# State-space products of a group: two runs of 14 with double-buffered decay matrices, or one run of 28 with four tiles

## The chip, the core and the metric

The kernel runs on one core of a Trainium2 chip. The time is that of the device for one execution, in microseconds. Before the change three runs took 1905.84, 1906.14 and 1908.29 us; the median is 1906.14.

## What is computed

Two transformer-like blocks run one after the other over 512 positions of width 1024. The change lies in the second block, in its state-space branch: 32 heads of width 64 in 8 groups of 4 heads; the heads of a group share two matrices B and C with 128 states. In the reference, cut to what matters:

```python
seg = a_cs[..., :, None] - a_cs[..., None, :]
decay_in = jnp.exp(jnp.where(causal, seg, -jnp.inf))
cb = jnp.einsum("bclgn,bcsgn->bgcls", c_mat, b_mat)
y_diag = jnp.einsum("bgcls,bgrcls,bcsgrp->bclgrp", cb, decay_in, xdt)
...
y_off = jnp.einsum("bclgn,bcgrpn,bgrcl->bclgrp", c_mat, prev, jnp.exp(a_cs))
y = y_diag + y_off + x * d_skip.reshape(G, R)[..., None]
```

So for every chunk and head there is a product of the inputs with a matrix "scores of B and C times the head's decay", and a product of C with the state carried in from the chunk before, scaled by a decay.

## The kernel before, in words

The second block keeps channels on the 128 partitions and positions on the free axis. Its large products go through `gemm_tile`: a weight block of 128 x 1024 values is loaded on SyncE's queue (`wr`, three buffers), split by ScalarE (`wh`, line 138) and VectorE (`wl`, line 139) into a high and a low part, and TensorE does three products of 128 x 512 for each of its eight slices (lines 150 to 152) into one of three accumulator banks (`acc`).

The state-space branch goes over 8 groups. For each group the loop calls `group_a` (line 873, the part that changes), then `group_in` for the next group (four gemms and short convolutions: two input tiles `xt`, B and C), the two gemms of a gated convolution, `z_in` (two gemms), one or two gate gemms, and `group_b`, which gates and normalises. The long convolution of 30 VectorE steps (line 826) is dealt out in the background.

`group_a` works with chunks of 128 positions, four of them. It transposes B and `xt` (lines 880, 887), scales the transposed inputs (`xd`, `xw`, line 891), forms the scores of B and C and masks them (`cb`, lines 897, 899), and builds the three carried states (`st`, lines 905 to 912). These use the two banks of the pool `mA`. Then it treats the heads in two pairs (e = 0, 1). For each head r of the pair a row of cumulated decays is loaded and broadcast to all partitions by a DMA on GpSimd's queue (`ab`, line 920, two buffers); ScalarE takes four Relus (line 924) and one Exp into another tile (`mt`, line 925, two buffers); VectorE multiplies by `cb` in place (line 926). A run of 14 products follows (line 935): 8 of `xd` with the factors into the bank `psd`, and 6 of C with the states into the bank `pso_`; both banks come from the pool `mB`, which has two. The two heads of a pair write the two halves of the partitions, so each product uses a tile of 128 x 64. Then VectorE assembles the pair's result `y` (lines 943 to 945), with a factor `ep` that a DMA loads (line 941).

The order of the work on each engine is fixed before the run by a planner: it simulates the engines with a cost model and gives each engine the ready instruction that was written first, or that has a raised priority (weight splitting has). `keep_in_program_order` ties an instruction behind the one written before it on its engine, so a run keeps its inner order; other products may still be placed between its members. A buffer of a tile's tag is given again when the last reader of its former content is done.

Of the kernel before, what the change touches and what calls it, by code (L numbers as in the profile page):

```python
# [6 lines left out]
F32 = mybir.dt.float32  # L7
# [3 lines left out]
AF = mybir.ActivationFunctionType  # L11
ALU = mybir.AluOpType
# [4 lines left out]
P = 128  # L17
# [51 lines left out]
def _build(tc, nc, es, a, out):  # L69
    V, A, T, G = nc.vector, nc.scalar, nc.tensor, nc.gpsimd  # L70
# [15 lines left out]
    def mA():  # L86
        return psa.tile([P, S], F32, tag="pa", name="pa")

    def mB():
        return psb.tile([P, S], F32, tag="pb", name="pb")  # L90
# [17 lines left out]
    mt = []  # L108
# [19 lines left out]
    def vcol(name, i=0, n=1):  # L128
        c, k = VEC[name]
        assert i + n <= k  # L130
        return vec[:, c + i:c + i + n]
# [146 lines left out]
    with es_mx:  # L278
# [6 lines left out]
        with tc.high_priority(2000):  # L285
            for k in range(0, 8, 2):
                c = slice(k, k + 2)
# [43 lines left out]
    with ExitStack() as ea:  # L331
# [9 lines left out]
        with ExitStack() as er:  # L341
# [11 lines left out]
                                 op0=ALU.mult, op1=ALU.add)  # L353
# [63 lines left out]
        ab = lambda i, j: 4 * i + j - i  # L417

        def hgrn_in(i):
            psf = gemm_tile([(a["w_gf"][i], 8)], xs)  # L420
            q = ph.tile([P, S], F32, tag="q", name="q")
            k_ = ph.tile([P, S], F32, tag="k", name="k")
            f = ph.tile([P, S], F32, tag="f", name="f")
            A.activation(out=f, in_=psf, func=AF.Sigmoid)
            psq = gemm_tile([(a["w_gq"][i], 8)], xs)
            sg = ph.tile([P, S], F32, tag="t", name="sg")
            A.activation(out=sg, in_=psq, func=AF.Sigmoid)
            V.tensor_scalar(out=f, in0=f, scalar1=oml[:, i:i + 1], scalar2=lb[:, i:i + 1], op0=ALU.mult, op1=ALU.add)
            V.tensor_scalar(out=k_, in0=f, scalar1=-1.0, scalar2=1.0, op0=ALU.mult, op1=ALU.add)
            V.tensor_tensor(out=q, in0=psq, in1=sg, op=ALU.mult)  # L430
            return q, k_, f
# [157 lines left out]
        hd = [hgrn_in(0), hgrn_in(1)]  # L589
# [7 lines left out]
        hd = [hgrn_in(2), hgrn_in(3)]  # L597
# [144 lines left out]
    acc_ = pdt.tile([P, 4, 32], F32, tag="acc_", name="acc_")  # L742
    wc = pdt.tile([P, 4, 32], F32, tag="wc", name="wc")
    cdb = pdt.tile([P, 32, 4], F32, tag="cdb", name="cdb")
    acsd = dram.tile([32, S], F32, tag="acsd", name="acsd")
# [127 lines left out]
    def group_a(g, xt, B, C):  # L873

        pg = pools["pg"]

        Bt = pg.tile([P, 3, P], F32, tag="Btok", name="Btok")
        ps = mA()
        for c in range(3):
            T.transpose(out=ps[:, c * P:(c + 1) * P], in_=B[:, c * P:(c + 1) * P], identity=ident)  # L880
        A.copy(out=Bt.rearrange("p a b -> p (a b)"), in_=ps[:, 0:3 * P])
        xd = pg.tile([P, 4, 4, 64], F32, tag="xd", name="xd")
        xw = pg.tile([P, 3, 4, 64], F32, tag="xw", name="xw")
        for e in range(2):
            ps = mA()
            for c in range(4):
                T.transpose(out=ps[:, c * P:(c + 1) * P], in_=xt[e][:, c * P:(c + 1) * P], identity=ident)  # L887
            pv = ps.rearrange("p (c r d) -> p c r d", r=2, d=64)
            hh = 4 * g + 2 * e
            for dst, sc, n in ((xd, dtc, 4), (xw, wc, 3)):  # L890
                V.tensor_tensor(out=dst[:, :, 2 * e:2 * e + 2, :], in0=pv[:, 0:n],
                                in1=sc[:, 0:n, hh:hh + 2].unsqueeze(3).to_broadcast([P, n, 2, 64]), op=ALU.mult)

        ps = mA()
        for c in range(4):
            sl = slice(c * P, (c + 1) * P)
            T.matmul(out=ps[:, sl], lhsT=B[:, sl], rhs=C[:, sl], start=True, stop=True)  # L897
        cb = pg.tile([P, 4, P], F32, tag="cb", name="cb")
        V.tensor_tensor(out=cb, in0=ps.rearrange("p (c l) -> p c l", l=P), in1=tri.unsqueeze(1).to_broadcast([P, 4, P]),
                        op=ALU.mult)  # L900

        st = pg.tile([P, 3, 256], F32, tag="st", name="st")
        for c in range(3):
            ps = mA()
            T.matmul(out=ps[:, 0:256], lhsT=Bt[:, c, :], rhs=xw[:, c].rearrange("p r d -> p (r d)"), start=True, stop=True)  # L905
            if c == 0:
                A.copy(out=st[:, 0, :], in_=ps[:, 0:256])
            else:
                V.tensor_tensor(out=st[:, c, :].rearrange("p (r d) -> p r d", d=64),
                                in0=st[:, c - 1, :].rearrange("p (r d) -> p r d", d=64),  # L910
                                in1=cdb[:, 4 * g:4 * g + 4, c].unsqueeze(2).to_broadcast([P, 4, 64]), op=ALU.mult)
                V.tensor_tensor(out=st[:, c, :], in0=st[:, c, :], in1=ps[:, 0:256], op=ALU.add)
        ys = []
        for e in range(2):
            psd = mB()
            mts = []
            for r in range(2):
                hd = 4 * g + 2 * e + r
                ab_ = pg.tile([P, 4, P], F32, tag="ab", name="ab", bufs=2)
                G.dma_start(out=ab_.rearrange("p a b -> p (a b)"), in_=acsd[hd:hd + 1, :].partition_broadcast(P))  # L920
                mt = pg.tile([P, 4, P], F32, tag="mt", name="mt", bufs=2)

                for c in range(4):
                    A.activation(out=ab_[:, c, :], in_=ab_[:, c, :], func=AF.Relu, scale=-1.0, bias=acc_[:, c, hd:hd + 1])
                A.activation(out=mt, in_=ab_, func=AF.Exp, scale=-1.0)
                V.tensor_tensor(out=mt, in0=mt, in1=cb, op=ALU.mult)
                mts.append(mt)


            pso_ = mB()  # L930
            run = [(psd, c, xd[:, c, 2 * e + r, :], mts[r][:, c, :], r) for c in range(4) for r in (1, 0)]
            run += [(pso_, c, st[:, c - 1, e * P + r * 64:e * P + r * 64 + 64], C[:, c * P:(c + 1) * P], r)
                    for c in range(1, 4) for r in (1, 0)]
            for i, (dst, c, lh, rh, r) in enumerate(run):
                m = T.matmul(out=dst[r * 64:r * 64 + 64, c * P:(c + 1) * P], lhsT=lh, rhs=rh, start=True, stop=True)  # L935
                if i:
                    tc.keep_in_program_order(m)
            ep = pg.tile([P, 3 * P], F32, tag="ep", name="ep", bufs=1)
            for r in range(2):
                hd = 4 * g + 2 * e + r  # L940
                G.dma_start(out=ep[r * 64:r * 64 + 64, :], in_=eacd[hd:hd + 1, P:].partition_broadcast(64))
            y = pg.tile([P, S], F32, tag="y", name="y", bufs=2)
            V.scalar_tensor_tensor(out=y, in0=xt[e], scalar=vcol("d_skip_2", 2 * g + e), in1=psd, op0=ALU.mult, op1=ALU.add)
            V.tensor_tensor(out=ep, in0=pso_[:, P:], in1=ep, op=ALU.mult)
            V.tensor_tensor(out=y[:, P:], in0=y[:, P:], in1=ep, op=ALU.add)
            ys.append(y)
        return ys
# [58 lines left out]
    for g in range(8):  # L1006
        ys = group_a(g, *cur)
        bg(BG[1])
        if g < 7:
            cur = group_in(g + 1)  # L1010
        bgq.append(conv31(g, glu(g)))
        bg(BG[3])
        zs = z_in(g)
        for _ in range(GPG[g]):
            gate_d(gq.pop(0))
            bg(BG[5])
        if g == 4:
            ssm_half(0, yn)
            yn = []
        yn += group_b(g, ys, zs)  # L1020
        bg(BG[6])
# [241 lines left out]
```

## Time and profile before

| what | value |
|---|---|
| median of three runs | 1906.14 us |
| profiled execution | 1905.93 us |
| its span, first to last instruction | 1904.2 us |
| TensorE matmul busy | 1882.7 us, 99% |
| VectorE busy | 1206.9 us, 63% |
| ScalarE busy | 861.9 us, 45% |
| GpSimd busy | 107.2 us, 6% |
| DMA, mean over the span | 111 GB/s |

Shares are of the span. PE is TensorE's matmul, PEld its weight load, DVE is VectorE, ACT is ScalarE, POOL is GpSimd. Matmuls are pipelined and their ends are modelled, so distances between starts tell more than durations. The state-space loop lies at about 855 to 1340 us of the span.

### The profile page before, as it was taken

To read this page: it belongs to the slowest core of one execution; us is meant where nothing else is said; L and a number is where in the kernel's file an instruction comes from. 1 tells how busy PE (TensorE), PEld (TensorE's weight loads), DVE (VectorE), ACT (ScalarE), POOL (GpSimd) and SP (SyncE) were. 2 spreads that over 40 slices of the span, in tenths; PEclk is the share of its full clock that TensorE was granted. 3 is DMA by queue.
4 is the path that set the end of the run, shared out by engine and by line. 5 is a ranking of instruction groups with operands and counts; after the bars stand their busy time and mean duration, and the time that the engine had idled before them with its cause. 6 is when DMAs were issued, how large, how long until landed. Compare 5 with 4: busy or idle time off the path is not lost.

```text
span 1904.2 us, 24959 instructions
## 1 busy us (share of the span) xinstructions
PE 1882.7 (99%) x9601; PEld 1563.1 (82%) x9601; DVE 1206.9 (63%) x1884; ACT 861.9 (45%) x1402; POOL 107.2 (6%) x207
## 2 busy tenths in 40 slices
PE   9999999999999999999999999999999999999997
PEld 8887776878888888877888888888888988888897
DVE  6744756665442344477988988579997764324456
ACT  6524556443431243358544663555344642232244
POOL 1001110000000000011110110110000000000000
PEclk9999999999999999999999999999999999999998
DMA  7312222312233223334433333332345522232244
GB/s 261 133 56 100 67 67 89 100 56 89 89 99 97 93 99 111 113 86 142 136 119 117 114 125 105 114 117 97 121 141 174 173 94 93 84 112 100 93 132 142
DMA packets 68511, 211.74 MB, mean 111 GB/s; under 512 B 8757, under 2 KB 15713, under 8 KB 68393
## 3 DMA queue, kind: packets, MB, share of 16 engines
q1 hardware_dynamic: 57856, 184.09, 29.4%
q0 software_dynamic: 6848, 19.75, 3.4%
q10 hardware_dynamic: 3688, 6.32, 1.0%
q8 instruction: 76, 1.25, 0.3%
q14 instruction: 43, 0.34, 0.1%
HBM read 201.59 MB, written 8.56 MB: 110 GB/s over the span
## 4 chain that ended last, share of the span: by engine, by line
PE 51%; issue 2%; DVE 1%; ACT 0%; DMA 0%; POOL 0%; POOLq 0%; DVEq 0%; ACTq 0%
PE acc L150 16%; PE acc L152 16%; PE acc L151 16%; PE pb L935 1%; PE pa L905 1%; PE pa L897 0%; PE pa L887 0%; PE pc L223 0%; DMA ab<-acsd 0%; PE pa L238 0%; PE pa L223 0%; POOL rc L231 0%; DVE yl L202 0%; PE pa L880 0%; DVE f L1175 0%
## 5 line engine op out<-in xcount | busy, mean ns | idle before, releaser
L138 ACT CAST wh<-wr 128x1024 fp32r<-128x1024 f32 (+1 forms) x343 | 347.2, 1013 | 720.8 <-PE acc L151 592.9
L139 DVE TENSOR_TENSOR wl<-wr,wh 128x1024 fp32r<-128x1024 f32 (+1 forms) x343 | 403.3, 1176 | 292.2 <-ACT wh L138 285.3
L150 PE MATMUL acc<-yh,wh 128*128 128x512 f32 (+1 forms) x1112 | 432.4, 389 | 0.4 <-DVE so L983 0.3
L152 PE MATMUL acc<-yh,wl 128*128 128x512 f32 (+1 forms) x1112 | 431.5, 388 | 0.0
L151 PE MATMUL acc<-yl,wh 128*128 128x512 f32 (+1 forms) x1112 | 429.8, 387 | 0.0
L152 PE MATMUL acc<-xh,wl 128*128 128x512 f32 (+1 forms) x832 | 314.4, 378 | 0.3 <-DVE wl L139 0.3
L151 PE MATMUL acc<-xl,wh 128*128 128x512 f32 (+1 forms) x832 | 313.5, 377 | 0.0
L150 PE MATMUL acc<-xh,wh 128*128 128x512 f32 (+1 forms) x832 | 313.1, 377 | 0.3 <-DVE h L613 0.3
L150 PEld LDWEIGHTS acc<-yh,wh 128*128 128x128 f32 x1112 | 209.1, 188 | 42.5 <-issue 1.4
L152 PEld LDWEIGHTS acc<-yh,wl 128*128 128x128 f32 x1112 | 209.0, 188 | 42.0 <-issue 1.2
L151 PEld LDWEIGHTS acc<-yl,wh 128*128 128x128 f32 x1112 | 209.1, 188 | 41.5 <-issue 1.1
L150 PE MATMUL acc<-uh,wh 128*128 128x512 f32 (+1 forms) x520 | 183.9, 354 | 0.0
L152 PE MATMUL acc<-uh,wl 128*128 128x512 f32 (+1 forms) x520 | 183.7, 353 | 0.0
L151 PE MATMUL acc<-ul,wh 128*128 128x512 f32 (+1 forms) x520 | 183.7, 353 | 0.0
L826 DVE SCALAR_TENSOR_TENSOR cv<-gp,vec,cv 128x512 f32<-128x512 f32 x240 | 177.9, 748 | 5.9 <-ACT cv L824 3.0
L152 PEld LDWEIGHTS acc<-xh,wl 128*128 128x128 f32 x832 | 157.3, 189 | 28.9 <-issue 2.4
L150 PEld LDWEIGHTS acc<-xh,wh 128*128 128x128 f32 x832 | 157.1, 189 | 28.6 <-ACT xh L201 0.9
L151 PEld LDWEIGHTS acc<-xl,wh 128*128 128x128 f32 x832 | 157.0, 189 | 27.3 <-issue 1.3
L150 PEld LDWEIGHTS acc<-uh,wh 128*128 128x128 f32 x520 | 98.3, 189 | 13.6
L152 PEld LDWEIGHTS acc<-uh,wl 128*128 128x128 f32 x520 | 98.3, 189 | 13.4
L151 PEld LDWEIGHTS acc<-ul,wh 128*128 128x128 f32 x520 | 98.3, 189 | 13.4
L231 POOL TENSOR_TENSOR rc<-rv,mhalf 128x4 f32<-128x4 f32 (+2 forms) x23 | 27.1, 1178 | 961.5 <-DVE rv L229 876.1
(370 smaller groups left out, 2095.8 us busy)
## 6 DMA issues: line engine op xcount, KB each, us to landing
wr<-w SPq DMA_DIRECT2D x64, 512.0 KB, 3.7
wr<-w_gu SPq DMA_DIRECT2D x44, 512.0 KB, 3.5
wr<-w_out SPq DMA_DIRECT2D x24, 512.0 KB, 3.5
wr<-w_dn SPq DMA_DIRECT2D x24, 512.0 KB, 3.5
wr<-w_xs SPq DMA_DIRECT2D x16, 512.0 KB, 3.5
wr<-w_glu SPq DMA_DIRECT2D x16, 512.0 KB, 3.8
ab<-acsd POOLq DMA_DIRECT2D x32, 256.0 KB, 3.8
wr<-w_z SPq DMA_DIRECT2D x16, 512.0 KB, 3.8
```

The costliest lines, as they stand in the source:

```text
L138: A.copy(out=hi[:, :n], in_=raw[:, :n])
L139: V.tensor_tensor(out=lo[:, :n], in0=raw[:, :n], in1=hi[:, :n].bitcast(F32), op=ALU.subtract)
L150: T.matmul(out=ps, lhsT=lh, rhs=rh, start=start, stop=False)
L151: T.matmul(out=ps, lhsT=lh, rhs=rl, start=False, stop=False)
L152: T.matmul(out=ps, lhsT=ll, rhs=rh, start=False, stop=stop)
L231: G.tensor_tensor(out=r[:, :nt], in0=v[:, :nt], in1=mhalf[:, :nt], op=ALU.pow)
L826: yield V.scalar_tensor_tensor(out=o, in0=gp[:, t:t + S], scalar=cw(t), in1=o, op0=ALU.mult, op1=ALU.add)
L905: T.matmul(out=ps[:, 0:256], lhsT=Bt[:, c, :], rhs=xw[:, c].rearrange("p r d -> p (r d)"), start=True, stop=True)
L935: m = T.matmul(out=dst[r * 64:r * 64 + 64, c * P:(c + 1) * P], lhsT=lh, rhs=rh, start=True, stop=True)
```

## The change

The four heads' decay matrices are worked out first, each in one tile of four (`ab`, four buffers; the tag `mt` is gone): load, Relu, Exp and multiplication all in place. Then one run has the products of all four heads: 16 products with the factors and 12 with the states, the pair e = 1 ahead of e = 0 in either part. The results go to four banks: the factor products to the two of `mB`, the state products to the two of `mA`. The loads of `ep` and the assembly of `y` follow for both pairs.

```diff
+        mts = []
+        for i in range(4):
+            hd = 4 * g + i
+            mt = pg.tile([P, 4, P], F32, tag="ab", name="ab", bufs=4)
+            G.dma_start(out=mt.rearrange("p a b -> p (a b)"), in_=acsd[hd:hd + 1, :].partition_broadcast(P))
+
+            for c in range(4):
+                A.activation(out=mt[:, c, :], in_=mt[:, c, :], func=AF.Relu, scale=-1.0, bias=acc_[:, c, hd:hd + 1])
+            A.activation(out=mt, in_=mt, func=AF.Exp, scale=-1.0)
+            V.tensor_tensor(out=mt, in0=mt, in1=cb, op=ALU.mult)
+            mts.append(mt)
+
+
+        psd, pso_ = [mB(), mB()], [mA(), mA()]
+        run = [(psd[e], c, xd[:, c, 2 * e + r, :], mts[2 * e + r][:, c, :], r)
+               for e in (1, 0) for c in range(4) for r in (1, 0)]
+        run += [(pso_[e], c, st[:, c - 1, e * P + r * 64:e * P + r * 64 + 64], C[:, c * P:(c + 1) * P], r)
+                for e in (1, 0) for c in range(1, 4) for r in (1, 0)]
+        for i, (dst, c, lh, rh, r) in enumerate(run):
+            m = T.matmul(out=dst[r * 64:r * 64 + 64, c * P:(c + 1) * P], lhsT=lh, rhs=rh, start=True, stop=True)
+            if i:
+                tc.keep_in_program_order(m)
         ys = []
         for e in range(2):
-            psd = mB()
-            mts = []
-            for r in range(2):
-                hd = 4 * g + 2 * e + r
-                ab_ = pg.tile([P, 4, P], F32, tag="ab", name="ab", bufs=2)
-                G.dma_start(out=ab_.rearrange("p a b -> p (a b)"), in_=acsd[hd:hd + 1, :].partition_broadcast(P))
-                mt = pg.tile([P, 4, P], F32, tag="mt", name="mt", bufs=2)
...
-            pso_ = mB()
-            run = [(psd, c, xd[:, c, 2 * e + r, :], mts[r][:, c, :], r) for c in range(4) for r in (1, 0)]
-            run += [(pso_, c, st[:, c - 1, e * P + r * 64:e * P + r * 64 + 64], C[:, c * P:(c + 1) * P], r)
-                    for c in range(1, 4) for r in (1, 0)]
...
-            V.scalar_tensor_tensor(out=y, in0=xt[e], scalar=vcol("d_skip_2", 2 * g + e), in1=psd, op0=ALU.mult, op1=ALU.add)
-            V.tensor_tensor(out=ep, in0=pso_[:, P:], in1=ep, op=ALU.mult)
+            V.scalar_tensor_tensor(out=y, in0=xt[e], scalar=vcol("d_skip_2", 2 * g + e), in1=psd[e], op0=ALU.mult, op1=ALU.add)
+            V.tensor_tensor(out=ep, in0=pso_[e][:, P:], in1=ep, op=ALU.mult)
```

## Rows read from the trace of the kernel before

**Rows 1.** The page: busy time by engine, granted TensorE clock in 40 slices.
```profile
PE 1882.7 (99%) x9601; PEld 1563.1 (82%) x9601; DVE 1206.9 (63%) x1884; ACT 861.9 (45%) x1402; POOL 107.2 (6%) x207
...
PEclk9999999999999999999999999999999999999998
```
**Rows 2.** TensorE's waits, 850 to 1345 us: who, for whom, total, times, longest.
```profile
PE pa L880 <- ACT Bt L804: 1.4, 1, 1.4
```
**Rows 3.** Line 935: instructions, ns min/median/max, first and last start, shapes.
```profile
L935 PE MATMUL pb<-mt,xd x256: 272/273/324, 874.2 to 1334.3; 128*64 128x128 f32 x128
...
L935 PE MATMUL pb<-Ct,st x192: 272/273/323, 875.1 to 1334.9; 128*64 128x128 f32 x192
```
**Rows 4.** Timeline (start, us, instruction): TensorE, gemm alone, 20 starts apart.
```profile
895.31 0.39 PE L150 MATMUL acc<-yh,wh 128*128 128x512 f32 x1
...
899.84 0.39 PE L152 MATMUL acc<-yh,wl 128*128 128x512 f32 x1
```
**Rows 5.** Timeline, TensorE, the runs of the first group.
```profile
875.12 0.61 PE L935 MATMUL pb<-Ct,st 128*64 128x128 f32 x8
...
875.99 0.39 PE L151 MATMUL acc<-yl,wh 128*128 128x512 f32 x1
...
877.15 0.39 PE L150 MATMUL acc<-yh,wh 128*128 128x512 f32 x1
877.47 0.44 PE L935 MATMUL pb<-Ct,st 128*64 128x128 f32 x4
...
878.17 0.39 PE L152 MATMUL acc<-yh,wl 128*128 128x512 f32 x1
...
880.47 0.39 PE L150 MATMUL acc<-yh,wh 128*128 128x512 f32 x1
880.78 1.09 PE L935 MATMUL pb<-mt,xd 128*64 128x128 f32 x16
881.71 0.82 PE L935 MATMUL pb<-Ct,st 128*64 128x128 f32 x12
...
882.80 0.39 PE L152 MATMUL acc<-yh,wl 128*128 128x512 f32 x1
```
**Rows 6.** Timeline, TensorE, the third group (980 to 1043 us).
```profile
986.95 0.40 PE L152 MATMUL acc<-yh,wl 128*128 128x512 f32 x1
987.28 1.09 PE L935 MATMUL pb<-mt,xd 128*64 128x128 f32 x16
...
988.96 0.50 PE L150 MATMUL acc<-yh,wh 128*128 128x512 f32 x1
...
991.82 1.09 PE L935 MATMUL pb<-mt,xd 128*64 128x128 f32 x16
```
**Rows 7.** Timeline, VectorE, the third group.
```profile
986.22 0.68 DVE L926 TENSOR_TENSOR mt<-mt,cb 128x512 f32<-128x512 f32 x1
...
987.80 0.42 DVE L912 TENSOR_TENSOR st<-st,pa 128x256 f32<-128x256 f32 x1
...
990.17 1.29 DVE L926 TENSOR_TENSOR mt<-mt,cb 128x512 f32<-128x512 f32 x2
```
**Rows 8.** Timeline, ScalarE, the third group; in brackets idle before and who ended it.
```profile
986.98 1.28 ACT L925 ACT_TABLE_LOAD   x1 [1.17 <-DVE mt L926]
988.41 1.16 ACT L925 ACTIVATE mt<-ab 128x512 f32<-128x512 f32 x2
...
993.33 1.27 ACT L924 ACTIVATE ab<-ab,acc__6602 128x128 f32<-128x128 f32 x4
...
996.84 0.63 ACT L925 ACTIVATE mt<-ab 128x512 f32<-128x512 f32 x1
997.49 1.28 ACT L804 ACT_TABLE_LOAD   x1
```
**Rows 9.** ScalarE's waits, 850 to 1345 us.
```profile
ACT wh L138 <- PE acc L151: 100.8, 49, 3.9
...
ACT ab L924 <- DMA ab<-acsd: 9.4, 9, 2.0
```
**Rows 10.** Timeline, GpSimd's queue, the third group.
```profile
989.34 0.60 POOL L920 DMA_DIRECT2D ab<-acsd  x1 [2.48 <-ACT mt L925]
```

More of the change, by code (lines that the diff above doesn't have):

```diff
@@ L913, in group_a @@
         ys = []
         for e in range(2):
-            psd = mB()
-            mts = []
-            for r in range(2):
-                hd = 4 * g + 2 * e + r
-                ab_ = pg.tile([P, 4, P], F32, tag="ab", name="ab", bufs=2)
-                G.dma_start(out=ab_.rearrange("p a b -> p (a b)"), in_=acsd[hd:hd + 1, :].partition_broadcast(P))
-                mt = pg.tile([P, 4, P], F32, tag="mt", name="mt", bufs=2)
[L923 to L927, printed above, removed]
@@ L930, in group_a @@
-            pso_ = mB()
-            run = [(psd, c, xd[:, c, 2 * e + r, :], mts[r][:, c, :], r) for c in range(4) for r in (1, 0)]
-            run += [(pso_, c, st[:, c - 1, e * P + r * 64:e * P + r * 64 + 64], C[:, c * P:(c + 1) * P], r)
-                    for c in range(1, 4) for r in (1, 0)]
[L934 to L937, printed above, removed]
```

## The prediction

> **What bounds the kernel now.** I read the busy shares first: TensorE is busy for 1882.7 of 1904.2 us and is granted full clock in nearly every slice [rows 1]. So an edit counts only by what it takes out of TensorE's own stream or puts into it as a gap. Next I read TensorE's waits in the state-space stage alone (850 to 1345 us): one of 1.4 us in the first group, where the transposes of B wait for its Silu, and one of 0.2 us that has no row here [rows 2]. All else the change touches (VectorE, ScalarE, GpSimd, DMA) works under cover there. Then I read line 935, the products of the heads: 256 + 192 = 448 instructions [rows 3]. A traced product of the source stands as two instructions, so these are 16 runs of 14 products, 28 instructions each; 15 stand whole, and the first one stands in two pieces, 24 + 4, with gemm products in between, so TensorE enters and leaves this kind of product 17 times. Last I read the timeline around single runs, where the reader is to look at starts only, since a matmul's end is modelled.
>
> **What one entry and exit costs.** Far from any run, gemm products start every (899.84 - 895.31)/20 = 0.2265 us [rows 4]. In the first group, from the gemm product ahead of a run to the second gemm product behind it, the whole run of 28 takes 882.80 - 880.47 = 2.33 us, the short piece of 4 takes 878.17 - 877.15 = 1.02 us [rows 5]. Their difference, 1.31 us for 24 instructions, is 0.0546 us for each; what is left of the short one is 1.02 - 4 x 0.0546 - 2 x 0.2265 = 0.35 us. This does not depend on the length of the run. The passage inside a run from the factor products to the state products (Ct) shows no such step: 16 instructions in 881.71 - 880.78 = 0.93 us, against 16 x 0.0546 = 0.87, and the 0.05 belongs to the entry. Behind the exit the gemm products limp a little: 875.99 to 877.15 is five steps in 1.16 us, 0.03 more than 5 x 0.2265. So one entry and exit is worth 0.38 us.
>
> Is that 0.35 a change of shape or a wait for data? The products' tile is 128\*64, the gemm's 128\*128. At 880.78 and at 877.47 nothing was being waited for by the timeline, and both pay the full sum; the runs of later groups, 987.28 among them, start 0.33 us behind the last gemm product, hardly more than the 0.31 to 0.32 of those two [rows 5, 6]. So at least nine tenths of it are the change of shape. The Trainium skill, page "TensorEngine Tiling (Array Packing)", section Tiling Modes, Key Properties, says that changing the tiling mode drains the engine while changing only the tile does not; by that rule merging runs saves the switches and nothing inside them, and the trace agrees: the passage inside a run is free.
>
> **The change part by part.**
> *Runs merged.* 17 entries and exits become 8, if each run of 28 products (56 instructions) stays whole: 9 x 0.38 = 3.4 us off TensorE's stream. The products' number and shape stay, 448 x 0.0546 = 24.5 us before and after. If switches vary as the measured ones do, 0.35 to 0.39, the term is 3.2 to 3.5.
>
> *One wait for four factors.* The first product of the new run reads the last factor (e = 1, r = 1), so one wait stands ahead of 56 instructions and of every gemm product queued behind them. Today the first run starts at 987.28, 0.38 us after its second factor ended at 986.90; the second pair's multiplications take 1.29 us, ended at 991.46, and the second run started at 991.82 [rows 6, 7]. Today's second pair is late because its Exp waits for the factor tiles that the first run reads: the table load at 986.98 and two Exps at 988.41 [rows 8]. With four tiles worked in place these Exps can be done long before, as today's first pair is, whose Exps stand at 995 to 997 for a run 50 us later. The run can then start some 1.3 us behind today's first, about 988.6, and 3 us ahead of today's second. TensorE needs 1.3 us of other work there; today it has 988.96 to 991.82, 2.9 us of gemm and one transpose, between the two runs, and only its place changes. I take zero. Bounds: below, zero, since there is no idle there to win back; above, 1.29 us for each of the 8 groups if the planner leaves the run where the first stands today, 10.3 us. I go by zero, since in all 16 present runs the planner's order met the data without a gap.
>
> *State products.* They read a state whose last addition ended at 988.22 [rows 7]; in the new run 32 instructions (1.75 us) come ahead of them. Cost zero; if the planner thinks the state late, as it did in the first group (row with x8), gemm products come in between and the run breaks: 0.38 us for each of 8, up to 3.0 us.
>
> *Banks.* The state products' results move to the pool that the transposes, the score products and the state updates use. The last of these is read by 988.22, ahead of the run, and the next use is the next group's transposes, 60 us on. Nothing else in the loop asks for that pool. Zero; if a bank is late it is the same break, 0.38 a group.
>
> *Loads.* All four 256 KB broadcasts of a group are freed by one run, and are issued together from GpSimd's queue, at 0.6 us each; today they come one by one, each released by an Exp, the first at 989.34 after 2.48 us of waiting in that queue [rows 10]. They will wait for TensorE instead. Behind them in that queue stand the loads of ep, the broadcast of the group norm and small memsets; TensorE waits for none of them in this stage today [rows 2]. ScalarE already waits for these broadcasts, 9.4 us in 9 times, longest 2.0 [rows 9]. More of that stays covered: ScalarE's weight casts wait for TensorE 100.8 us in 49 times [rows 9], so ScalarE is ahead of the products by whole blocks. Zero, bounds -1.4 (the idle of the first group goes) to +4.5 (below).
>
> *Tables.* Four Exps instead of two lie outside the run's neighbourhood, and between them Silu of the next group's convolutions. Today's one pair of loads a group (986.98 and 997.49, 1.28 us each) may become two pairs: 2.57 us more of ScalarE a group, where it has 100.8 us of waiting over 8 groups. I take zero. The Trainium skill, page "ScalarE: Activation LUTs", section What ACT_TABLE_LOAD costs, puts a switch at about 2.66 us, 1.28 for the load and 1.38 for a drain, and speaks against scattering Exps; the load agrees, the drain does not: the load at 997.49 starts 0.02 us behind the end of the Exp (996.84 + 0.63) [rows 8]. By the Trainium skill's figure a second pair would be 5.3 us a group; the measured one decides.
>
> **Sum.** The profiled execution took 1905.93 us, 1.73 outside its span; less 3.4 is 1902.5. It lies 0.2 below the median of the three runs shown; on the median, 1906.14 - 3.4 = 1902.7. What a measurement of this kernel can tell from no change is 0.2%, 3.8 us, so the gain as worked out stays just inside it.
>
> **Rivals.**
> *Broken runs.* The planner puts gemm products between the two parts of every run: 1902.7 + 8 x 0.38 = 1905.7. For it: the first group did that. Against: 15 of 16 did not, and more work now lies ahead of the state products. 12%.
>
> *The one wait (slower).* The run is queued about where today's first run stands and TensorE stands for the second pair of factors: 8 x 1.29 = 10.3 us, 1913.0. The gain is gone from 0.43 us of standing a group; slower by over 0.2% from 0.9. For it: one instruction holds 56, and the order is fixed ahead of time. Against: no present run shows a gap. 8%.
>
> *First group.* There ScalarE gates TensorE [rows 2], the broadcasts land late, and four heads' work is free to start. If one head's four Relus (1.27), an Exp (0.63) and two loads (2.57) come ahead of the Silu of B, TensorE stands 4.5 us longer: 1907.2. Against: program order gives the Silus the earlier place. 8%. The other way, the order shifts so that the 1.4 us of idle goes: 1901.3. 12%.
>
> *Nothing hidden shows:* eight whole runs, no new gap: 1902.7, itself 1902.0 to 1903.4. 60%.
>
> **How the numbers follow.** Broken runs, the forecast and the better first group make 84%; 1900.8 to 1906.2 holds them with half a microsecond to spare, and I take off 4% for shifts of the planner's order that I can't price. Faster by over 0.2% means below 1902.33: the better first group and a third of the forecast's own range, 0.32. Slower means above 1909.95: the one wait, and a little for unpriced shifts, 0.10. The rest, 0.58, is within.
>
> **What would show it.** Line 935 in 8 unbroken stretches of 56, each from the gemm product ahead to the second behind in 0.35 + 56 x 0.0546 + 0.453 = 3.86 us; no TensorE wait for VectorE's line 926; Exps of all four heads ahead of the score products; the second pair of multiplications directly behind the first on VectorE. Wrong: stretches of 32 and 24, a TensorE idle ended by VectorE's factor at the head of a run, or a longer idle ahead of the first transposes of B.

## The result, and the profile after

The changed kernel takes 1918.98 us (median of 4 runs, 1918.58 to 1919.11), the kernel before 1905.99: the ratio is 1.0065, with a 95% interval of 1.0049 to 1.0081. So it is slower by some 13 us, where 3.4 us of gain was forecast. The profiled execution took 1919.06 us, 13.13 more than that of before.

The page's busy row answers to [rows 1]; ScalarE grew by 912.9 - 861.9 = 51.0 us.

```profile
PE 1886.7 (98%) x9601; PEld 1570.4 (82%) x9601; DVE 1206.4 (63%) x1884; ACT 912.9 (48%) x1442; POOL 107.3 (6%) x207
```

TensorE's waits from 850 to 1460 us (who, for whom, us in total, times, longest; two under 0.5 are left out). The kernel before has one of 1.4 us [rows 2] and, behind 1345 us, two of 0.3 and 0.4:

```profile
PE pc L223 <- DVE sqa L215: 3.7, 2, 2.5
PE acc L150 <- ACT xt L800: 3.2, 1, 3.2
PE pa L880 <- ACT Bt L804: 2.4, 1, 2.4
PE acc L150 <- ACT wh L138: 1.5, 1, 1.5
```

The run itself went nearly as worked out. It is line 932 now; the timeline of TensorE (start, us) in the third group, which answers to [rows 6]:

```profile
996.05 0.48 PE L151 MATMUL acc<-yl,wh 128*128 128x512 f32 x1
996.46 1.97 PE L932 MATMUL pb<-ab,xd 128*64 128x128 f32 x32
998.26 1.48 PE L932 MATMUL pa<-Ct,st 128*64 128x128 f32 x24
999.67 0.50 PE L152 MATMUL acc<-yh,wl 128*128 128x512 f32 x1
1000.01 0.40 PE L150 MATMUL acc<-yh,wh 128*128 128x512 f32 x1
```

All eight runs stand whole, 56 instructions each. From the gemm product ahead (996.05) to the second behind (1000.01) are 3.96 us, where 3.86 was worked out; the products from 996.46 to 999.67 are 3.21 of it, 56 x 0.0546 = 3.06 and 0.15. To see what a group gains, I lay the two traces side by side at the first transpose of B (line 880) of each group; the figure is its start in the changed kernel less that in the kernel before, in us:

| | first group | 2nd | 7th | 8th | end of span |
|---|---|---|---|---|---|
| changed kernel | 1.71 | 7.58 | 5.70 | 9.70 | 13.13 |
| e1 (below) | 0.38 | -1.09 | -2.20 | -2.59 | 0.69 |
| e2 (below) | 1.41 | 1.44 | -0.44 | -0.81 | 4.90 |
| e4 (below) | -0.55 | 3.59 | 2.11 | 1.74 | 5.29 |
| e8 (below) | -0.01 | -1.49 | -3.27 | -3.66 | -4.48 |
| e10 (below) | -0.51 | 3.76 | 1.89 | 4.58 | 4.85 |
| e11 (below) | 0.69 | 0.64 | -1.24 | -1.64 | -0.86 |

From the second group to the seventh the changed kernel gains 1.88 us in five groups, 0.376 each: one entry and exit less in each, as forecast (0.38). The loss is in three places: 5.9 us between the first and second group's transposes, with 1.1 more ahead of them; 4.0 in the seventh; 3.4 in the eighth and behind it.

In the first group TensorE waits for a bank that ScalarE empties late, and then the run of 56 takes 885.96 - 881.21 = 4.75 us where it takes 3.21 elsewhere:

```profile
869.88 0.55 PE L880 MATMUL pa<-ident,Bt 128*128 128x128 f32 x3 [2.42 <-ACT Bt L804]
...
880.71 0.57 PE L150 MATMUL acc<-yh,wh 128*128 128x512 f32 x1 [3.16 <-ACT xt L800]
881.21 3.52 PE L932 MATMUL pb<-ab,xd 128*64 128x128 f32 x32
884.55 1.48 PE L932 MATMUL pa<-Ct,st 128*64 128x128 f32 x24
885.96 0.50 PE L151 MATMUL acc<-yl,wh 128*128 128x512 f32 x1
```

The run is longer because of the clock. Busy time by stretch, changed kernel; the third figure from the right is the granted clock:

```profile
870.80:874.10 3.30, 3.30 (x13) 2.67 (x12) 2.31 (x4) 3.27 (x7) 0.00 (x0) 0.50 0.43 151
881.10:884.30 3.20, 3.20 (x31) 3.10 (x32) 2.83 (x4) 2.29 (x4) 0.82 (x2) 0.50 0.39 148
884.50:887.80 3.30, 3.30 (x36) 2.82 (x33) 3.00 (x6) 2.13 (x6) 1.17 (x4) 1.00 0.73 232
1273.60:1276.90 3.30, 3.30 (x11) 2.72 (x11) 2.61 (x5) 0.12 (x1) 0.10 (x1) 0.50 0.35 113
1335.00:1338.30 3.30, 3.30 (x14) 2.91 (x13) 1.68 (x4) 0.00 (x0) 0.00 (x0) 0.50 0.50 161
```

Behind each of four idles in the stage TensorE ran 3.41 us at the lower level, 1.2 GHz (870.77 to 874.18, 881.01 to 884.42, 1273.54 to 1276.95, 1334.98 to 1338.39): some 1.7 us more per idle, an estimate from half the stretch; the run above lost 1.54 in one. The account: new idles 1.07 + 3.16 + 2.52 + 1.17 + 1.13 = 9.05 (the first is 2.42 less the 1.35 of before, the last, 1.45 at 1443 us, less 0.32), half clock 4 x 1.7 = 6.8, merged runs -3.4, and 0.65 that the profiled runs differed by ahead of the stage: 13.1.

Who made ScalarE and VectorE late? In the first group it is not the number of table loads: as in the kernel before, two stand there ahead of the run (865.62 and 871.61; before 863.90 and 869.90). Two other things changed. The first decay load, one of four issued together now, took longer to land (7.3 us from its issue, before 5.7), so ScalarE started later (before, then changed kernel):

```profile
861.79 1.57 ACT L924 ACTIVATE ab<-ab,acc__6602 128x128 f32<-128x128 f32 x5 [2.01 <-DMA ab<-acsd]
```
```profile
863.50 1.58 ACT L920 ACTIVATE ab<-ab,acc__6602 128x128 f32<-128x128 f32 x5 [3.08 <-DMA ab<-acsd]
```

That is the 1.07 us more of idle ahead of the transposes. And the third and fourth head's Exps and the fourth head's Relus now stand ahead of the reading at line 800 that empties the gemm's bank; this is the idle of 3.16 us. Before, the third Exp came at 875.37, behind that reading. ScalarE, before and changed:

```profile
873.33 0.78 ACT L800 ACTIVATE xt<-acc,vec 128x512 f32<-128x512 f32 x1
```
```profile
879.36 0.63 ACT L921 ACTIVATE ab<-ab 128x512 f32<-128x512 f32 x1
879.89 0.76 ACT L800 ACTIVATE xt<-acc,vec 128x512 f32<-128x512 f32 x1
```

In the later groups the table loads come in. Those from 850 to 1345 us, changed kernel (count, busy us, mean ns, idle before them); before there were 9 at line 925 and 9 at line 804:

```profile
L921 ACT ACT_TABLE_LOAD x29 | 37.2, 1283 | 0.5
L804 ACT ACT_TABLE_LOAD x22 | 28.2, 1283 | 0.3
L869 ACT ACT_TABLE_LOAD x8 | 10.3, 1283 | 0.1
```

59 instead of 18: 41 x 1.283 = 52.6 us, and the busy row grew by 51.0. In the third group's period ScalarE has eight of them, where [rows 8] had two (the first two and the last are shown):

```profile
1004.52 1.28 ACT L921 ACT_TABLE_LOAD   x1
1005.82 0.64 ACT L921 ACTIVATE ab<-ab 128x512 f32<-128x512 f32 x1
...
1006.98 1.28 ACT L804 ACT_TABLE_LOAD   x1
...
1035.33 1.28 ACT L869 ACT_TABLE_LOAD   x1
```

From the second group to the sixth they cost TensorE nothing, as the gain of 0.376 a group shows. Ahead of the seventh group's transposes the slack was used up: ScalarE comes later to line 824, VectorE works on its result and is late with the squares (`sqa`), and TensorE waits for these at line 223. Changed kernel, then before:

```profile
1258.35 1.28 ACT L921 ACT_TABLE_LOAD   x1
...
1260.18 0.80 ACT L824 ACTIVATE cv<-gp,vec 128x512 f32<-128x512 f32 x1
1271.87 0.69 DVE L215 TENSOR_TENSOR sqa<-sqa,sq 128x512 f32<-128x512 f32 x1
1272.61 1.05 PE L223 MATMUL pc<-ones,sqa 128*128 128x1 f32 x8 [2.52 <-DVE sqa L215]
```
```profile
1250.06 0.82 ACT L824 ACTIVATE cv<-gp,vec 128x512 f32<-128x512 f32 x1 [1.31 <-DVE gp L817]
1262.55 0.69 DVE L215 TENSOR_TENSOR sqa<-sqa,sq 128x512 f32<-128x512 f32 x1
```

TensorE's own lag is 5.7 us there; line 824 lags by 10.1 and `sqa` by 9.3.

The four Exps now stand one by one between the Silus of the next group's convolutions (line 804) and of z (line 869). Before, an Exp could not go ahead until one of two `mt` tiles was free, which kept Exps together around the runs; four tiles in place are all free behind the run, and the planner puts each Exp where ScalarE is ready for it. That reason is read from the code and the order; no run varies the number of tiles alone. ScalarE's slack, its waits from 850 to 1345 us, fell with it against [rows 9]:

```profile
ACT wh L138 <- PE acc L151: 46.1, 16, 3.9
...
ACT ab L920 <- DMA ab<-acsd: 24.6, 7, 4.3
```

### The profile page after: what moved, and what is told of

It reads as the page before. It is cut to its first block, busy times and chain, and to the rows that moved or that the text cites. A ratio compares the mean times of both kernels' runs of the same rounds, so it can differ in the third digit from the quotient of the medians.

```text
span 1917.3 us, 24971 instructions
## 1 busy us (share of the span) xinstructions
PE 1886.7 (98%) x9601; PEld 1570.4 (82%) x9601; DVE 1206.4 (63%) x1884; ACT 912.9 (48%) x1442; POOL 107.3 (6%) x207
## 4 chain that ended last, share of the span: by engine, by line
PE 46%; issue 3%; DVE 3%; ACT 2%; DMA 1%; POOL 0%; POOLq 0%; DVEq 0%; ACTq 0%
PE acc L150 14%; PE acc L152 14%; PE acc L151 14%; PE pb L932 1%; DVE cv L826 1%; DVE wl L139 1%; PE pa L905 1%; PE pa L932 1%; ACT wh L138 0%; PE pa L897 0%; PE pa L887 0%; DMA ab<-acsd 0%; PE pc L223 0%; ACT cv L1038 0%; PE pa L238 0%
```

## The experiments

All edits are to the changed kernel; ratios are to the kernel before, run on the same chip, with their 95% interval. The theories at the start: A, the scattered Exps (their table loads hold ScalarE, and that TensorE); B, the four loads issued at once; C, the merged run. They ran on several chips, and the kernel before took 1905.0 to 1905.5 us beside them.

**e1: the Exps kept together.** Each Exp is tied behind the copy of the group's first state, which stands shortly ahead of the run.

```diff
-                A.copy(out=st[:, 0, :], in_=ps[:, 0:256])
+                cp = A.copy(out=st[:, 0, :], in_=ps[:, 0:256])
...
-            A.activation(out=mt, in_=mt, func=AF.Exp, scale=-1.0)
+            with tc.issue_after(cp.ins):
+                A.activation(out=mt, in_=mt, func=AF.Exp, scale=-1.0)
```

> The changed kernel with one thing more: the four Exps of every group are tied behind the copy of the group's first state on ScalarE (the copy at line 907), so they can't be placed among the next group's Silus. Theory A (the scattered Exps bring 41 more table loads, 1.283 us each, and these hold ScalarE up where TensorE depends on it): 18 table loads in the state-space stage instead of 59, the TensorE idles of 2.5, 1.2 and 1.5 us in the last two groups and behind the loop shrink to those of the kernel before, the saving of 0.38 us a run stays: 1902 to 1905 us (up to 1907 if the four Exps right ahead of the run make it wait). Rival B (the four loads freed together by one run land late, and ScalarE waits for them): loads are as bunched as before, so 1912 or more. Rival C (the single run of 28 and its one wait): 1915 or more.

1906.62 us, ratio 1.0011 (1.0002 to 1.0020): 12.4 of the 13 us come back. 16 table loads are left in the stage, and the first group's and the seventh's loss are gone. From the second group's transposes on, the gain is 0.36 to 0.39 in each group but the third, where a wait of 0.47 us for VectorE at line 897 takes it away. So the scattered Exps are shown as the cause there; whether by their loads or by their places, this run can't tell. But from the eighth group's transposes to its run's end 4.4 us are lost, so that none of the gain is left. VectorE's `sqa` and TensorE behind it, timelines of e1:

```profile
1320.69 0.69 DVE L215 TENSOR_TENSOR sqa<-sqa,sq 128x512 f32<-128x512 f32 x1
```
```profile
1321.44 1.05 PE L223 MATMUL pc<-ones,sqa 128*128 128x1 f32 x8 [2.19 <-DVE sqa L215]
```

VectorE is late, TensorE stands 2.19 us, and has half clock from 1323.5 to 1327.0.

**e2: no table loads, same places.** Tanh stands in for Exp, so the decay matrices are not the reference's; the other instructions stay, and the table need not change.

```diff
-            A.activation(out=mt, in_=mt, func=AF.Exp, scale=-1.0)
+            A.activation(out=mt, in_=mt, func=AF.Tanh, scale=-1.0)
```

> The changed kernel with Tanh in place of Exp at line 921, so that it needs no other table than Silu and Tanh (the decay matrices are then not those of the reference). Loads, Relus, run and banks stay. Theory A: hardly a table load is left in the state-space stage, ScalarE is 50 us less busy than in the changed kernel, and the time falls to 1901 to 1906 us, with what the first group still loses. Rival B: 1915 or more, since the loads stay bunched. Rival C: 1915 or more, since the run stays.

1909.21 us, 1.0023 (1.0012 to 1.0033); one table load is left in the stage. 9.8 us come back: the seventh group's loss is gone, and of the first group's two idles of 2.4 and 3.2 us there are left 1.8 and 1.1, with no half clock behind them. But Tanh removes 17 table loads that the kernel before has too, so the 9.8 us are not the price of the 41 new ones alone. The 3 us above what was expected are again in the last group: line 223 waits 2.0 us there, with half clock behind it, for 6.83 us this time.

**e3: four tiles in place, but two runs of 14.** The runs are written as before the change, with their banks from `mB`.

```diff
+            psd[e], pso_[e] = mB(), mB()
+            run = [(psd[e], c, xd[:, c, 2 * e + r, :], mts[2 * e + r][:, c, :], r) for c in range(4) for r in (1, 0)]
```

> The changed kernel with the merged run alone undone: four tiles in place, all four heads worked out first, but two runs of 14 products into the banks of before. Theory A: the Exps can still be scattered, so table loads stay well above 18 and the time stays above the kernel before, 1910 to 1923 us (16 entries and exits instead of 8 cost 3 us more than the changed kernel). Rival C: the loss goes with the merged run, 1906 us. Rival B: the loads are freed by two runs in pairs, so about half the loss stays, 1911 to 1914.

1911.79 us, 1.0040 (1.0025 to 1.0055): slower than before without the merged run, so C alone is not the cause. The time lies in the ranges of A and of B, and does not tell them apart. It shows the rival of broken runs at work instead. TensorE, third group:

```profile
990.98 1.09 PE L934 MATMUL pb<-ab,xd 128*64 128x128 f32 x16
991.90 0.61 PE L934 MATMUL pb<-Ct,st 128*64 128x128 f32 x8
992.44 0.50 PE L150 MATMUL acc<-yh,wh 128*128 128x512 f32 x1
...
993.57 0.44 PE L934 MATMUL pb<-Ct,st 128*64 128x128 f32 x4
```

From the second group on the first run stands in pieces of 24 and 4: 23 entries instead of 17, and each group loses 0.33 us where the changed kernel gains 0.376. Its other loss is mostly in the first group. It has 33 table loads, fewer than the changed kernel's 59, and no wait at line 223.

**e4: Exps tied in all groups but the first.**

```diff
+            with tc.issue_after(cp.ins) if g > 0 else ExitStack():
```

> As the first of these, but the Exps are tied only in groups 1 to 7; the first group is left as the changed kernel has it. Theory A, with the loss split by place from the two traces (first group 6.9 us of idle and half clock, the last two groups and what follows about 8): 1910 to 1912 us. If the first group's loss also comes from the later groups' order, 1905 or less; rivals B and C: 1917 or more.

1912.00 us, 1.0044 (1.0029 to 1.0058): against e1 5.4 us are lost, and TensorE's wait of 3.2 us for the bank in the first group is back. So the place of the first group's four Exps alone is worth about that. The stage has 16 table loads, as in e1: it is the place of the Exps and not more loads. The wait ahead of the first transposes is 1.4 us, as in the kernel before, so the 1.07 us more of the changed kernel's profiled run is not always there.

**e5: e1 with the loads behind Rg's.** What holds VectorE in e1 is a transfer. Its wait there from 850 to 1345 us (3.3 us in two times before):

```profile
DVE zs L965 <- DMA Rg<-rd: 21.9, 7, 4.1
```

Rg, the broadcast of the group norm, is issued among the four decay loads (`far` lists its loads). Theory D: it comes late because it stands behind loads that wait for the run's end. Rival E: VectorE lacks time in the last, shorter group anyway.

```diff
+            with tc.issue_after(far[n_far + g - 2].ins) if g > 1 else ExitStack():
                 G.dma_start(out=mt.rearrange("p a b -> p (a b)"), in_=acsd[hd:hd + 1, :].partition_broadcast(P))
```

> As e1 (each group's two Exps tied behind the copy of its state, table loads few), and besides, for the groups from 2 on, the four decay loads are put behind the load of Rg (VectorE's gated norm, two groups back) in GpSimd's queue. Theory D (in e1 VectorE is held 3 to 4 us a group by Rg's load, which stands behind decay loads that wait for the end of the run; so VectorE is late with sqa in the last group and TensorE waits 2.2 us at col_sum and then runs 3.4 us at half its clock): the wait at line 223 in group 7 goes, and with it 4.4 us: 1902.0 to 1903.5. Rival E (VectorE has no time to spare in the last, shorter group whatever Rg's load does): the wait stays, 1906 to 1908.

1908.03 us, 1.0016 (1.0005 to 1.0027), no better than e1 (in its profiled run the transposes of B in the first group waited 2.2 us, where e1's waited 0.8). VectorE's wait for Rg fell, but another load, `ep`, took its place:

```profile
DVE ep L947 <- DMA ep<-eacd: 11.9, 6, 3.0
DVE zs L968 <- DMA Rg<-rd: 8.6, 7, 2.7
```

It did not tell D from E, because it moved only one of two loads.

**e6: e1 with the column sum later.** Line 223 of the seventh group's norm gets a lower priority, so TensorE reaches it just ahead of the run.

```diff
-        with tc.high_priority(-APRI):
+        with tc.high_priority(-APRI if g < 6 else -2 * APRI):
```

> As e1, and besides only the column sum of group 6 (the product at line 223 that waited 2.2 us for VectorE in e1) is given a later place in TensorE's order, just before the state-space run. Nothing is done for VectorE. If the rest of e1's loss (4.4 us in the last group) is that one wait at the head of TensorE's queue and the half clock behind it, the time is 1902 to 1903.5, and runs of line 933 stay at 0.36 us of fixed cost. If VectorE is late for everything in that group, another wait of TensorE for it takes the place of this one and the time stays at 1905 to 1908.

1906.53 us, 1.0010 (1.0001 to 1.0018). The wait at line 223 is gone, and in its place the transposes wait 2.1 us for ScalarE, which stands behind VectorE in the same norm:

```profile
1322.34 0.66 PE L887 MATMUL pa<-ident,xt 128*128 128x128 f32 x4 [2.10 <-ACT Btok L881]
```

So VectorE's lateness is the cause, not the place of one product.

**e7: the loads behind Rg's, Exps left scattered.** e5's edit alone.

> The changed kernel with the decay loads of groups 2 on put behind Rg's load in GpSimd's queue, and the Exps left where they were (scattered, some 50 to 60 table loads in the stage). Theory A (the table loads on ScalarE are the main cost): most of the loss stays, 1912 to 1919. If the place of the decay loads in GpSimd's queue were the main cost: 1903 to 1908.

1914.51 us, 1.0043 (1.0029 to 1.0058): the wait of 3.2 us for the bank in the first group is there, line 223 waits 2.9 us in two times, and 47 table loads are left.

**e8: e1 with the loads behind ep's and Rg's.** The decay loads of a group go behind the last `ep` load of the group before, which stands behind Rg's.

```diff
-                G.dma_start(out=ep[r * 64:r * 64 + 64, :], in_=eacd[hd:hd + 1, P:].partition_broadcast(64))
+                eps.append(G.dma_start(out=ep[r * 64:r * 64 + 64, :], in_=eacd[hd:hd + 1, P:].partition_broadcast(64)))
...
+            with tc.issue_after(eps[4 * g - 1].ins) if g else ExitStack():
                 G.dma_start(out=mt.rearrange("p a b -> p (a b)"), in_=acsd[hd:hd + 1, :].partition_broadcast(P))
```

> As e1 (Exps tied behind the copy of the state), and the four decay loads of a group put behind the last ep load of the group before in GpSimd's queue, so behind Rg's load too: nothing that VectorE reads stands any more behind decay loads that wait for the end of the run. In e5 only Rg's load was moved ahead and the ep load took its place as VectorE's wait (3.0 us between the transposes of groups 6 and 7). Theory D (these 3 us are why VectorE's sqa, TensorE's col_sum and the half clock are late in group 7): VectorE's waits for Rg and ep fall under 1 us there, the wait of 2.2 us at line 223 goes, 1902.0 to 1903.5. Rival E (VectorE has too little time in the last group whatever the loads do): line 223 still waits 1.5 us or more, 1906 to 1908.

1903.92 us (11 runs, 1901.43 to 1905.16), 0.9990 (0.9981 to 0.9998): faster than both kernels, though by little: the medians lie 1.1 us apart, a third of the gain that was forecast. GpSimd's queue in the seventh group, and TensorE at the head of the eighth, which doesn't wait:

```profile
1272.93 0.60 POOL L251 DMA_DIRECT2D Rg<-rd  x1 [5.58 <-DMA rd<-rt]
1276.86 1.04 POOL L944 DMA_DIRECT2D ep<-eacd  x2 [3.33 <-DVE y L948]
...
1277.92 2.17 POOL L920 DMA_DIRECT2D ab<-acsd  x4
```
```profile
1317.59 0.60 PE L889 MATMUL pa<-ident,xt 128*128 128x128 f32 x4
1318.02 0.95 PE L223 MATMUL pc<-ones,sqa 128*128 128x1 f32 x8
```

E falls: VectorE had the time, once no load held it. From the second group's transposes to the eighth's it gains 2.17 us, 0.36 a group. From the product at line 778, ahead of the stage, to the end of the span the profiled run gains 4.48 - 0.80 = 3.7 us, against the 3.4 worked out; but that execution, 1901.45 us, is the second fastest of the eleven, and 0.6 us of it is a shorter wait ahead of the first transposes.

**e9: e1 with the decay loads on SyncE's queue.**

```diff
-            G.dma_start(out=mt.rearrange("p a b -> p (a b)"), in_=acsd[hd:hd + 1, :].partition_broadcast(P))
+            nc.sync.dma_start(out=mt.rearrange("p a b -> p (a b)"), in_=acsd[hd:hd + 1, :].partition_broadcast(P))
```

> As e1, with the four decay loads issued from SyncE's queue between the weight loads instead of GpSimd's. Theory D: GpSimd's loads (Rg, ep) no longer stand behind them, VectorE's wait for Rg goes and line 223 does not wait, 1902 to 1903.5, unless the weight loads behind them come late, which would show as ScalarE's casts or TensorE waiting for wr. Rival E: line 223 still waits 1.5 us or more in group 7, 1906 to 1908.

1907.36 us, 1.0013 (1.0003 to 1.0022): neither. Nothing stood ahead of Rg in GpSimd's queue any more, yet VectorE waited 12.5 us for Rg and 10.5 for `ep`, and line 223 2.4 us. So D as I put it, the place in the queue, is only a part: VectorE's wait for Rg falls from 21.9 to 12.5 us by it. The rest goes with the loads being in flight together; how they hold each other up, no run shows. The rows of DMA issues, 850 to 1345 us (times, KB, median us from issue to landing), before, e1, e9 and e8:

```profile
Rg<-rd POOLq DMA_DIRECT2D x7, 256.0 KB, 4.7
```
```profile
Rg<-rd POOLq DMA_DIRECT2D x7, 256.0 KB, 6.0
```
```profile
Rg<-rd POOLq DMA_DIRECT2D x7, 256.0 KB, 5.5
```
```profile
Rg<-rd POOLq DMA_DIRECT2D x7, 256.0 KB, 4.3
```

In e9 the first decay load is issued at 1273.58 and Rg's at 1274.11, and Rg lands as late as in e1, or nearly; in e8 Rg goes alone and lands as soon as before. The Trainium skill, page "DMA: Bandwidth & Descriptors", section Issuing engines are not separate DMA queues, says that transfers started by different engines run on the same 16 DMA engines and interleave; e9 agrees, 5.5 us.

**e10 and e11: the two causes apart.** e10 is e8's order of loads with the Exps left scattered; e11 the same with Tanh for Exp (not the reference's result).

> The changed kernel with its Exps left where they were (59 table loads in the stage or about as many) and only the decay loads put behind the last ep load, as in e8. If the two causes add (table loads some 8 to 9 us in the groups before the last, the decay loads' place some 4 us in the last one): 1913 to 1916. If the place of the loads is nothing by itself: 1917 to 1920. If it is the main cost after all: below 1909.

> As e2 (Tanh in place of Exp, so no table loads and a result that is not the reference's; the instructions stand where the changed kernel has them) and the decay loads behind the last ep load, as in e8. If table loads and late loads are the whole loss: 1902 to 1905, with no wait at line 223 in the last group. If the order of ScalarE's scattered instructions costs something by itself, apart from the table loads: 1906 to 1910.

e10 takes 1911.60 us, 1.0031 (1.0019 to 1.0042); e11 1904.84, 0.9999 (0.9990 to 1.0009). So of the changed kernel's 1919.0, the order of loads alone gives back 7.4, the table loads alone (e2) 9.8, both 14.1. That is 3.1 less than their sum; probably (no run shows it apart) each removes a part of VectorE's delay in the last two groups that the other would remove too. e10 came out 1.4 us better than I expected, for the same reason if so. In e11 line 223 waits no more; what TensorE still waits for is ScalarE in its scattered order (1.5 us for `wh`, 1.3 for `Bt`, 1.1 for line 800, from 850 to 1460 us), some 3 us more than in e8.

The table of starts now tells the causes apart by place. Between the first and second group's transposes the changed kernel loses 5.9 us, e4 4.1 and e10 4.3; e1, e8, e2 and e11 lose nothing: the place of the first group's Exps, with the loads that go with it. In the seventh group it loses 4.0 and e10 2.7, while e1, e2, e4, e8 and e11 gain 0.4: the new table loads, to which the order of the loads adds some. Behind the eighth group's transposes it loses 3.4, e1 3.3, e2 5.7 and e4 3.6, while e8 gains 0.8 and e10 and e11 lose 0.3 and 0.8: the order of the loads. So B is a part of the cause, by what it does to VectorE's other loads, and C is none.

## Why the prediction was wrong

- *One entry and exit, 0.38 us; 9 fewer.* Right: 0.376 a group over five groups, and all eight runs whole. The changed kernel's runs pay 0.08 us more at six of eight entries (3.95 us instead of 3.87 from gemm product to gemm product); e1's don't, and the gain of a group is no smaller for it.
- *One wait for four factors, state products, banks: zero.* Right. No run waits for a factor or breaks; the state products follow inside it (998.26 above). The rivals of broken runs and of the one wait did not happen.
- *Tables: "may become two pairs: 2.57 us more of ScalarE a group, where it has 100.8 us of waiting over 8 groups. I take zero."* This is the step that failed: work of ScalarE in a new order was priced at nothing. The four Exps became up to four pairs: 41 loads more, 52.6 us or 6.6 a group. From the second group to the sixth zero was right even so; in the seventh, where ScalarE and VectorE were late by then, they cost 4.0 us and the group's gain (gone in e1, e2 and e4). And a sum of waits over eight groups was set against them, though the wait of [rows 2] showed that ScalarE had no slack in the first group. What failed there is the order and not the count: two Exps and four Relus more ahead of line 800, 3.2 us of idle with half clock behind it; e4 puts the first group at 5.4 us. The Trainium skill, page "ScalarE: Activation LUTs", section What ACT_TABLE_LOAD costs, counts a cost for every switch of tables; of its two parts the load, 1.283 us, agrees again, and 41 more of it account for the growth of the busy row, while the drain is not seen here either: the load at 1004.52 ends at 1005.80 and the Exp starts at 1005.82.
- *Loads: "Zero, bounds -1.4 ... to +4.5".* Failed too, inside its bounds. I asked who waits for what stands behind them in the queue, and only of TensorE. VectorE waits, and TensorE for VectorE a norm later: 4.4 us in e1's last group, of which e8 gives back 4.1. The 1.07 us ahead of the first transposes is a late load as well, though not in every run.
- *The price of an idle.* Not in the sum at all: each of the four new idles in the stage brought 3.41 us of half clock, some 6.8 us on 9.05 of idle.
- *Rival "first group" (1907.2).* It had the place, the engine and one of the signs named (a longer idle ahead of the first transposes, 2.42 us). That its 4.5 us of idle lie near the 4.2 measured is luck: no Exp and no table load more came ahead of the Silu of B, but a load landed late (1.07), and Exps came ahead of line 800 (3.16). It lacked the half clock (3.4 us) and the other groups.
- *Bounds.* The scatter could have been asked for ahead: the two `mt` tiles held the Exps back [rows 8], and the change takes them away. Priced as four pairs a group, 6 more loads x 1.283 x 8 = 61.6 us, it would have been a term with a bound of its own.

Open: why the planner scatters Exps and Silus (only that it does is shown); where the idle of 1.45 us at 1443 us comes from (e2, e10 and e11 have it, e1 and e8 have not); and why e8's median lies 2.5 us above its profiled run (1901.45), whose trace shows no stretch of half clock ahead of the last 10 us. Runs of one kernel differ by such amounts, and only one of each was profiled. At 362 us, where the code is the same, the profiled run of the kernel before has a stretch of half clock and that of e8 has none, so part of such differences may be the clock.

## What to carry to other kernels

A buffer that is short may be what keeps an engine's instructions in a good order; when a change frees it, ask what the scheduler will do with the freedom, and count the table loads of the new order. Slack is read at the place where it is needed, not as a sum over the stage. When transfers are released together, look at everyone who waits for another transfer at that time, on whatever queue it was issued, and follow that engine to the bound.

## What the runs showed of the hardware

An idle of TensorE cost more than itself: behind idles of 2.42, 3.16, 2.52 and 1.17 us the granted clock was 0.50 for 3.41 us, and 56 products took 4.75 instead of 3.21 us. But the idle of 1.4 us in the kernel before [rows 2] had no such stretch behind it, nor had one of 1.8 us in e2 and one of 1.9 us in e9, so the length of the idle alone does not decide.

A 256 KB broadcast took 4.3 us from issue to landing (median of 7) when issued alone (e8) and 6.0 among four others of its size (e1); with those four issued from another engine's queue it was 5.5 (e9).
